# Spreading the last gate's adaLN rows over both MLP products, with their loads issued by GpSimd

## The chip, the core and the metric

The kernel runs on one core of a Trainium2 chip. Five engines of that core work side by side and meet only at semaphores: TensorE (PE; PEld is its weight load), VectorE (DVE), ScalarE (ACT), GpSimd (POOL) and SyncE (SP), which here only issues DMAs. Each runs its own list of instructions in a fixed order. The metric is the device time of one execution in microseconds (us). The times before are 1996.33, 1995.65 and 1997.18 us: a median of 1996.33.

## The reference, cut to what matters

One decoder layer on 512 tokens of width 2048, all in float32:

```python
mod = (c_act @ w_ada[l] + b_ada[l]).reshape(B, 6, D)
sh1, sc1, gt1, sh2, sc2, gt2 = [mod[:, j][:, None, :] for j in range(6)]
...
h = rmsnorm(x, g_norm_mlp[l]) * (1.0 + sc2) + sh2
hid = jnp.square(jax.nn.relu(jnp.einsum('bsd,df->bsf', h, w_mlp_in[l])))   # 2048 -> 8192
y = jnp.einsum('bsf,fd->bsd', hid, w_mlp_out[l])                           # 8192 -> 2048
x = x + gt2 * y
return rmsnorm(x, g_norm_final)
```

`gt2`, the last gate, is a product of the conditioning vector with 2048 columns of `w_ada`. Nothing needs it before the first finished columns of the second MLP product.

## The kernel before

**Arithmetic.** float32 products run as three matmuls each on a high and a low part (a*w = ah*wh + al*wh + ah*wl), so every weight tile is split first: ACT copies the high part, DVE subtracts it to get the low one (`low`, L122). Both MLP products use the Strassen-Winograd scheme: seven products instead of eight on half matrices. One **set** (one turn of the loop in `strassen`) loads one 512 KB weight tile `raw` (L1058, issued by SP), lets DVE form four sums of weights (L1060, L1067, L1068, tile `ts`), splits both (ACT L1066 and L1072; DVE L122, once 768 and once 1024 columns wide) and then runs 42 matmuls of 128x256 (L1102 to L1104) into seven PSUM banks.

**First product.** The hidden dimension is done in groups of 512 columns. Group 0 goes another way; groups 1 to 15 are 8 sets each. After a group, `combine` (one ACT copy, L1113, and seven DVE additions, L1114 to L1120) takes the seven banks apart; the next group needs those banks. There are eight. Squared-ReLU, splits and the sums for the second product follow in the background as `keep_parts` (L940, L948, L949: stores to DRAM issued by POOL) or, for the last two groups, `hold_parts` (kept in SBUF).

**Second product.** 13 parts of 8 to 16 sets (`parts`) walk over four blocks of output columns. A part that does not finish its block copies its seven banks out (L397 on ACT, L399 on DVE) and stores them as `prod` (L1300, POOL); a later part of the same block loads five of them back into tiles `n` (`load_pre`, L1239, POOL) and ACT puts them into the banks (L1090). The hidden activations come back from DRAM as pairs (`load_pair`, L1141 and L1144 on SP), split by ACT L1151 and DVE L122. The first three parts need no reload. The fourth part, 16 sets long, does the fourth block; the reload for the fifth part is asked for at its start.

**The last gate.** `ada_late` works through 64 **rows**: a row is a 128x512 tile of the transposed `w_ada` (256 KB), multiplied by the conditioning vector and summed by one DVE instruction (L1203). After every fourth row two tiny DVE instructions (L1208, L1209) finish 128 values of the gate. Three rows are loaded ahead (`LEAD`), into tiles `n`, of which there are five, in SP's queue. `ada_late` is a generator in the background lane `bg2`: each `tick()` (one per set) takes one off the lane's `wait`, and each row adds `pace[0]` to it, so the pace is in sets per row. `ensure(GT2)` runs what is left at once.

**Order.** The order on each engine comes from the tile framework's scheduler: it follows the program's order with priorities (`SETW` = 200 for the split of weights, `SETE` = 330 for `combine` and the copies out of the banks, rows at none) and its own estimate of when operands are there. DMAs under `keep_in_program_order` keep their order among themselves. The lines below show both functions and what calls them.

Of the kernel before, what the change touches and what calls it, by code (L numbers as in the profile page):

```python
# [16 lines left out]
P = 128  # L17
S = 512
D = 2048
NK = D // P  # L20
# [19 lines left out]
SH1, SC1, GT1, SH2, SC2, GT2 = range(6)  # L40
# [24 lines left out]
def hybrid_layer_kernel(  # L65
# [13 lines left out]
    nc = tc.nc  # L79
# [18 lines left out]
    def T(tag, dt=F32, cols=None):  # L98
        return new(next(split_tag) if tag == "w4" else tag, dt, cols)

    def new(tag, dt=F32, cols=None):
        count[0] += 1
        pool, bufs = (sp, BUFS[tag]) if tag in BUFS else pools[tag][:2]
        return pool.tile([P, cols or COLS[tag]], dt, tag=tag, name=f"{tag}_{count[0]}", bufs=bufs)

    def bank(tag):
        count[0] += 1
        return pp.tile([P, S], F32, tag=tag, name=f"ps_{tag}_{count[0]}", bufs=PBUFS[tag])
# [39 lines left out]
    def col(base, j):  # L148
        return vec[:, base + j : base + j + 1]
# [23 lines left out]
    for i in range(2):  # L173
        v = slice(i * S, (i + 1) * S)
        ps = bank("mm")
# [7 lines left out]
    def mod(m, j):  # L183
        return mods[:, m * NK + j : m * NK + j + 1]
# [80 lines left out]
    def blk(o):  # L265
        return slice(o * P, (o + 1) * P)


    class Lane:
# [8 lines left out]
        def next(self):  # L278
            if not self.queue:
                return False  # L280
            try:
                self.wait += next(self.queue[0]) or 0.0
            except StopIteration:
                self.queue.pop(0)
            return True
# [13 lines left out]
    bg, bgl, bg2 = Lane(), Lane(), Lane()  # L299

    def tick(dt=1.0):
        for lane in (bg, bgl, bg2):
            lane.run(dt)
# [137 lines left out]
    for o in range(8):  # L441
        t = T("a")
# [266 lines left out]
    pace = [3.2]  # L709

    def ensure(m):
        while m not in ready:
            assert bg2.next()
# [339 lines left out]
    def operands(src):  # L1053

        with tc.high_priority(offset=SETW):

            r = T("raw")
            nc.sync.dma_start(r.rearrange("p (c f) -> p c f", c=2), src)  # L1058
            t = T("ts")
            tt(  # L1060
                out=t[:, : 2 * HT].rearrange("p (a b) -> p a b", a=2),
                in0=r[:, HT : 3 * HT].rearrange("p (a b) -> p a b", a=2),
                in1=r[:, q_(0)].unsqueeze(1).broadcast_to([P, 2, HT]), op=ALU.add,
            )
            h, lo = T("w3", F32R), T("w3", F32R)
            act(h, r[:, HT:], AF.Copy)  # L1066
            tt(out=t[:, q_(2)], in0=t[:, q_(0)], in1=r[:, q_(2)], op=ALU.add)  # L1067
            tt(out=t[:, q_(3)], in0=t[:, q_(2)], in1=r[:, q_(3)], op=ALU.add)  # L1068
            low(lo, r[:, HT:], h)
            out = {n: (h[:, q_(i)], lo[:, q_(i)]) for i, n in enumerate(("11", "22", "21"))}  # L1070
            h, lo = T("w4", F32R), T("w4", F32R)
            act(h, t, AF.Copy)  # L1072
            low(lo, t, h)
            for i, n in enumerate(("t1", "t3", "t2", "t4")):
                out[n] = h[:, q_(i)], lo[:, q_(i)]
        return out
# [3 lines left out]

    loaded = [None]

    def strassen(src, acts, after=None, pre=None, before=None, js=range(8)):

        bs = [bank(next(turn)) for _ in PRODUCTS]
        if pre:
            n, ts = pre
            with tc.high_priority(offset=SETE):
                for b, t in zip(bs, ts):
                    act(b, t, AF.Copy)  # L1090
                for b, t in zip(bs[5:], load_pre(n, (5, 6), nc.scalar)):
                    act(b, t, AF.Copy)
        if before:
            loaded[0] = before()
        for j in js:
            w, a = operands(src(j)), acts(j)
            for b, (an, wn) in zip(bs, PRODUCTS):
                (ah, al), (wh, wl) = a[an], w[wn]
                for i in range(2):
                    out, st = b[:, q_(i)], j == js[0] and i == 0 and not pre  # L1100
                    kw = dict(skip_group_check=True)
                    mm(out, wh[:, blk(i)], ah, start=st, stop=False, **kw)  # L1102
                    mm(out, wh[:, blk(i)], al, start=False, stop=False, **kw)  # L1103
                    mm(out, wl[:, blk(i)], ah, start=False, stop=j == js[-1], **kw)  # L1104
            if after:
                after(j)
            tick()
        return bs
# [71 lines left out]
    at = itertools.count(-8)  # L1180

    def after_set():
        for f, p in todo.get(next(at), []):
            f(p)

    LEAD, row = 3, ["n"]

    def ada_late(m):

        def load(i):  # L1190
            t = T(row[0])
            tc.keep_in_program_order(nc.sync.dma_start(t, w_adaT[(m * NK + i // 4) * P : (m * NK + i // 4 + 1) * P, i % 4 * S : (i % 4 + 1) * S]))
            return t

        ts = [load(i) for i in range(LEAD)]
        for i in range(4 * NK):
            t, q = ts.pop(0), i % 4
            if i + LEAD < 4 * NK:
                ts.append(load(i + LEAD))
            yield pace[0]  # L1200
            if q == 0:
                ga = T("ga")
            stt(  # L1203
                out=t, in0=t, scalar=1.0, in1=cb[q // 2][:, q % 2 * S : (q % 2 + 1) * S], op0=ALU.mult, op1=ALU.mult,
                accum_out=ga[:, q : q + 1],
            )
            if q == 3:
                tt(out=ga[:, :2], in0=ga[:, :2], in1=ga[:, 2:4], op=ALU.add)  # L1208
                stt(  # L1209
                    out=mod(m, i // 4), in0=ga[:, 0:1], scalar=ga[:, 1:2], in1=col(C_BADA, m * NK + i // 4),  # L1210
                    op0=ALU.add, op1=ALU.add,
                )
        ready.add(m)

    pace[0] = 1.9
    w_pair = w_mlp_in.rearrange("(c k p) f -> k p c f", c=2, p=P)
    for g in range(1, NG):
        if g == 2:
# [2 lines left out]
        bs = strassen(lambda j: w_pair[j][:, :, g * 512 : (g + 1) * 512], acts_in, last, js=range(KP)[:: -1 if g == 1 else 1])  # L1221
# [5 lines left out]
        bg.add((keep_parts if g < NG - 2 else hold_parts)(g, *rs))  # L1227


    row[0] = "a"  # L1230
    prodD = [[dp.tile([P, S], F32, name=f"prod_{n}_{i}") for i in range(7)] for n in range(NO)]
    w_blocks = w_mlp_out.rearrange("(g c b p) d -> g b p c d", c=2, b=2, p=P)
    x2 = {}
# [2 lines left out]
    def load_pre(n, js, queue=nc.gpsimd):  # L1236
        ts = [T("n") for _ in js]
        for t, j in zip(ts, js):
            queue.dma_start(t, prodD[n][j])  # L1239
        return ts  # L1240
# [9 lines left out]
    nxt = None  # L1250
# [6 lines left out]
    for i, (n, ps) in enumerate(parts):  # L1257
        seen = {m for m, _ in parts[: i + 1]}
        left = [m for m, _ in parts[i + 1 :]]

        def before():
            if left and left[0] in seen:
                return left[0], load_pre(left[0], range(5))

        def after(p, n=n, early=(ps[4],) if n not in left and n < NO - 1 else ()):
            after_set()
            if p in early:
                load_x2(range(n * 4, n * 4 + 4), x1D)
            if i == len(parts) - 1 and p == ps[5]:
                load_x2(range(12, NK), x1D)  # L1270

        src = lambda q: w_blocks[ORDER[q] // 2][ORDER[q] % 2][:, :, n * 512 : (n + 1) * 512]
        bs = strassen(src, acts_out, after, nxt, before, ps)
        nxt = loaded[0]
        if n not in left:
            ensure(GT2)
            cs = [T("cb"), T("cb")]
            qs = [t[:, j * S : (j + 1) * S] for t in cs for j in range(2)]
            with tc.high_priority(offset=SETE):
                qs = combine(bs, *qs)  # L1280
            if n == NO - 1:
                for q, d in zip(qs, yD):
                    nc.gpsimd.dma_start(d, q)
                continue
            if acc2 is None:
                acc2 = T("a")
            with tc.high_priority(offset=SETW):
                for k, tok, q in quarters(n, *qs):
                    t = x2[k][:, tok]
                    stt(out=t, in0=q, scalar=mod(GT2, k), in1=t, op0=ALU.mult, op1=ALU.add)  # L1290
                for k, q in zip(range(n * 4, n * 4 + 4), qs):
                    add_square(acc2, x2[k], q, k == 0)
                    if n == 0:
                        nc.gpsimd.dma_start(x2D[k], x2[k])
        else:
            with tc.high_priority(offset=SETE):
                for j, b in enumerate(bs):
                    t = T("a")
                    copy(j + 1, t, b)
                    nc.gpsimd.dma_start(prodD[n][j], t)  # L1300
# [12 lines left out]
    for p in final:  # L1313
        t = T("a", F32R)
# [154 lines left out]
```

## Time and profile before

| | |
|---|---|
| median of three runs | 1996.33 us (1995.65 to 1997.18) |
| the profiled execution's own time | 1994.49 us |
| its span, first to last instruction | 1992.7 us |
| PE busy | 1941.9 us (97%) |
| DVE busy | 1760.6 us (88%) |
| ACT busy | 1074.6 us (54%) |
| POOL busy | 193.6 us (10%) |
| mean granted TensorE clock | 0.996 |
| moved by DMA | 443.51 MB, mean 223 GB/s |

The profile is one execution taken by the hardware profiler. "Busy" is a union of instruction times of one engine. In a window row, the number in brackets after an engine is its count of instructions in the window; a few matmul records can be missing. In a timeline row, the two first numbers are start and duration in us, and a bracket at the end tells how long the engine stood idle before it and what released it. The groups 1 to 15 of the first product run from about 760 to 1355 us, the second product from there to about 1960 us.

### The profile page before, as it was taken

The page shows a single profiled execution, that of the slowest core. Times are in us where ns is not written, and L with a number is a line of the kernel's source. Part 1 is how long each engine was busy: PE and PEld are TensorE (multiplying, and loading weights), DVE is VectorE, ACT ScalarE, POOL GpSimd, SP SyncE. Part 2 cuts the span into 40 slices and gives each one's busy share as a digit, 9 for nine tenths or more (in the row PEclk, how much of TensorE's full clock was granted, in tenths as well). Part 3 has the DMA queues.
Part 4 walks back from the last instruction along what each step waited for, and adds up shares of the span by engine and source line. Part 5 has one row for each costly group of instructions (what it writes and reads, how often), then busy time and mean ns, then how long its engine had stood idle before and what let it go on. Part 6 is the DMA issues. An engine that isn't in the chain of part 4 may idle for free. (4 is left out here: it accounts for less than half of the span.)

```text
span 1992.7 us, 37203 instructions
## 1 busy us (share of the span) xinstructions
PE 1941.9 (97%) x14148; PEld 1815.3 (91%) x14148; DVE 1760.6 (88%) x2979; ACT 1074.6 (54%) x1580; POOL 193.6 (10%) x307
## 2 busy tenths in 40 slices
PE   8999999999999998999999999999999999999997
PEld 6787887788888998999999999999999999999996
DVE  8998776988998599999999999999879779879996
ACT  5443564786433385555555555556445555556552
POOL 0000000000000000112111211200110210211100
PEclk9999999999999999999999999999999999999998
DMA  9896655556779544766666665755567668679653
GB/s 368 304 340 198 212 163 185 179 163 218 226 251 365 170 134 129 239 194 213 221 196 203 226 197 190 232 173 210 185 241 262 238 249 278 220 253 341 225 197 112
DMA packets 205238, 443.51 MB, mean 223 GB/s; under 512 B 20481, under 2 KB 42113, under 8 KB 205058
## 3 DMA queue, kind: packets, MB, share of 16 engines
q1 hardware_dynamic: 176338, 356.58, 54.2%
q0 software_dynamic: 23680, 77.61, 10.5%
q10 hardware_dynamic: 5040, 6.93, 1.0%
q8 instruction: 111, 1.82, 0.4%
q14 instruction: 69, 0.57, 0.1%
HBM read 376.30 MB, written 64.75 MB: 221 GB/s over the span
## 5 line engine op out<-in xcount | busy, mean ns | idle before, releaser
L1102 PE MATMUL ps_mm<-a,w 128*128 128x256 f32 x1696 | 469.1, 277 | 3.0 <-DVE a L1114 1.2
L1104 PE MATMUL ps_mm<-a,w 128*128 128x256 f32 x1696 | 469.2, 277 | 0.4 <-DVE w L122 0.3
L1103 PE MATMUL ps_mm<-a,w 128*128 128x256 f32 x1696 | 469.1, 277 | 0.4 <-DVE a L122 0.3
L1072 ACT ACTIVATE w<-ts 128x1024 fp32r<-128x1024 f32 x244 | 258.4, 1059 | 273.1 <-DVE ts L1068 241.5
L1104 PE MATMUL ps_z<-a,w 128*128 128x256 f32 x1304 | 362.0, 278 | 6.9 <-DVE w L122 6.8
L1102 PE MATMUL ps_z<-a,w 128*128 128x256 f32 x1304 | 362.2, 278 | 3.4 <-DVE a L1118 1.6
L1103 PE MATMUL ps_z<-a,w 128*128 128x256 f32 x1304 | 361.4, 277 | 0.1
L122 DVE TENSOR_TENSOR w<-ts,w 128x1024 fp32r<-128x1024 f32 x244 | 297.8, 1221 | 55.4 <-PE ps_mm L1103 20.4
L1102 PEld LDWEIGHTS ps_mm<-a,w 128*128 128x128 f32 x1696 | 318.4, 188 | 4.3 <-issue 2.5
L1104 PEld LDWEIGHTS ps_mm<-a,w 128*128 128x128 f32 x1696 | 318.7, 188 | 1.1 <-DVE w L122 1.0
L1103 PEld LDWEIGHTS ps_mm<-a,w 128*128 128x128 f32 x1696 | 318.7, 188 | 0.8 <-DVE a L122 0.8
L122 DVE TENSOR_TENSOR w<-raw,w 128x768 fp32r<-128x768 f32 (+1 forms) x296 | 267.5, 905 | 37.8 <-ACT w L244 24.0
L1066 ACT ACTIVATE w<-raw 128x768 fp32r<-128x768 f32 x244 | 204.5, 839 | 174.8 <-issue 80.5
L1104 PEld LDWEIGHTS ps_z<-a,w 128*128 128x128 f32 x1304 | 245.6, 189 | 8.2 <-DVE w L122 8.1
L1102 PEld LDWEIGHTS ps_z<-a,w 128*128 128x128 f32 x1304 | 245.8, 188 | 4.9 <-issue 2.1
L1103 PEld LDWEIGHTS ps_z<-a,w 128*128 128x128 f32 x1304 | 245.7, 188 | 0.6 <-DVE a L122 0.6
L244 ACT ACTIVATE wh<-wr 128x512 fp32r<-128x512 f32 (+1 forms) x184 | 113.2, 618 | 142.4 <-PE ps_mm L262 61.8
L1060 DVE TENSOR_TENSOR ts<-raw 128x512 f32<-128x512 f32 x244 | 166.8, 684 | 14.2 <-DMA raw<-in_w_mlp_out_dram 13.4
L259 PE MATMUL ps_mm<-a,wh 128*128 128x512 f32 x448 | 176.8, 395 | 2.6 <-DVE a L460 1.0
L263 PE MATMUL ps_mm<-a,wl 128*128 128x512 f32 x448 | 175.0, 391 | 1.5 <-DVE wl L122 1.3
L262 PE MATMUL ps_mm<-a,wh 128*128 128x512 f32 x448 | 174.9, 390 | 0.0
L211 DVE SCALAR_TENSOR_TENSOR x<-x,cb 128x1024 f32<-128x1024 f32 x108 | 131.2, 1218 | 23.4 <-DMA x<-in_w_adaT_dram 23.3
(336 smaller groups left out, 4007.7 us busy)
## 6 DMA issues: line engine op xcount, KB each, us to landing
raw<-in_w_mlp_out_dram SPq DMA_DIRECT2D x124, 512.0 KB, 4.6
raw<-in_w_mlp_in_dram SPq DMA_DIRECT2D x120, 512.0 KB, 3.8
x<-in_w_adaT_dram SPq DMA_DIRECT2D x108, 512.0 KB, 5.6
wr<-in_w_in_dram SPq DMA_DIRECT2D x160, 256.0 KB, 3.4
tt<-in_w_adaT_dram SPq DMA_DIRECT2D x52, 512.0 KB, 6.2
part<-a POOLq DMA_DIRECT2D x84, 256.0 KB, 3.9
a<-part SPq DMA_DIRECT2D x84, 256.0 KB, 6.3
prod<-a POOLq DMA_DIRECT2D x63, 256.0 KB, 5.8
```

What stands on the lines that cost most here:

```text
L122: tt(out=out, in0=full, in1=f32(high), op=ALU.subtract)
L211: ins = stt(out=t, in0=t, scalar=1.0, in1=cb[q_], op0=ALU.mult, op1=ALU.mult, accum_out=self.ga[:, q_ : q_ + 1],)
L244: act(h[:, :n], r[:, :n], AF.Copy)
L259: first = mm(out, wh, ah, start=start, stop=False, **kw)
L262: mm(out, wh, al, start=False, stop=False, **kw)
L263: mm(out, wl, ah, start=False, stop=stop, **kw)
L1060: tt(out=t[:, : 2 * HT].rearrange("p (a b) -> p a b", a=2), in0=r[:, HT : 3 * HT].rearrange("p (a b) -> p a b", a=2), in1=r[:, q_(0)].unsq ...
L1066: act(h, r[:, HT:], AF.Copy)
L1072: act(h, t, AF.Copy)
L1102: mm(out, wh[:, blk(i)], ah, start=st, stop=False, **kw)
L1103: mm(out, wh[:, blk(i)], al, start=False, stop=False, **kw)
L1104: mm(out, wl[:, blk(i)], ah, start=False, stop=j == js[-1], **kw)
```

## The change

Four things change, all around the 64 rows of the last gate:

- the pace in the first product is 2.7 sets per row instead of 1.9, and in the second product 1.3; at the start of the second product the lane waits 5 sets more;
- the row loads are issued by POOL instead of SP, always into tiles `n` (before, the last two went into tiles `a`);
- the reload for the fifth part is asked for at the 13th set of the fourth part instead of its first;
- `ensure(GT2)` moves from the first finished block to that reload.

```diff
-    def strassen(src, acts, after=None, pre=None, before=None, js=range(8)):
+    def strassen(src, acts, after=None, pre=None, before=None, js=range(8), at=0):
...
-        if before:
-            loaded[0] = before()
-        for j in js:
+        for n_, j in enumerate(js):
+            if before and n_ == at:
+                loaded[0] = before()
             w, a = operands(src(j)), acts(j)
...
-    LEAD, row = 3, ["n"]
+    LEAD, ROWS = 3, (2.7, 1.3)
...
-            t = T(row[0])
-            tc.keep_in_program_order(nc.sync.dma_start(t, w_adaT[...]))
+            t = T("n")
+            tc.keep_in_program_order(nc.gpsimd.dma_start(t, w_adaT[...]))
...
-    pace[0] = 1.9
+    pace[0] = ROWS[0]
...
-    row[0] = "a"
+    pace[0] = ROWS[1]
+    bg2.wait += 5.0
...
         def before():
             if left and left[0] in seen:
+                ensure(GT2)
                 return left[0], load_pre(left[0], range(5))
...
-        bs = strassen(src, acts_out, after, nxt, before, ps)
+        bs = strassen(src, acts_out, after, nxt, before, ps, 12 if i == 3 else 0)
         nxt = loaded[0]
         if n not in left:
-            ensure(GT2)
```

Because a scheduler sets the order, the diff does not tell where instructions end up. Three places show it. The first is DVE at the end of group 10 of the first product, up to the first addition of `combine` (L1114). `n_...` with L1203 is a row, `w_...` a split of weights. Before:

```order
L122 TENSOR_TENSOR w_2326_12785<-raw_12780,w_2325_12784 128x768
L1060 TENSOR_TENSOR ts_12857<-raw_12855 128x512
L1203 SCALAR_TENSOR_TENSOR n_12978,ga_13161<-n_12978,cb_82 128x512
L1067 TENSOR_TENSOR ts_12857<-ts_12857,raw_12855 128x256
L1068 TENSOR_TENSOR ts_12857<-ts_12857,raw_12855 128x256
L122 TENSOR_TENSOR w_2328_12791<-ts_12782,w_2327_12790 128x1024
L122 TENSOR_TENSOR w_2337_12860<-raw_12855,w_2336_12859 128x768
L1114 TENSOR_TENSOR a_12763<-ps_z_12256,a_12761 128x512
```

and now:

```order
L122 TENSOR_TENSOR w_2312_12743<-raw_12738,w_2311_12742 128x768
L1060 TENSOR_TENSOR ts_12815<-raw_12813 128x512
L1067 TENSOR_TENSOR ts_12815<-ts_12815,raw_12813 128x256
L1068 TENSOR_TENSOR ts_12815<-ts_12815,raw_12813 128x256
L122 TENSOR_TENSOR w_2314_12749<-ts_12740,w_2313_12748 128x1024
L122 TENSOR_TENSOR w_2323_12818<-raw_12813,w_2322_12817 128x768
L1114 TENSOR_TENSOR a_12721<-ps_z_12217,a_12719 128x512
```

The row that stood five instructions ahead of the combine is gone from this stretch. Between the combines of groups 1 to 15 DVE's list had 3, 8, 7, 4, 4, 4, 5, 4, 4, 4, 4, 5, 4 and 2 rows (the first number is what stands ahead of group 2's combine); now it has 3, 6, 3, 3, 3, 3, 3, 3, 3, 3, 3, 3, 7 and 1. Of the rows that are left, 17 come in the second product, in bunches.

The second place is POOL's queue at the end of the third part of the second product, from the last store of that part's banks on. Before:

```order
L1300 DMA prod_6_15434<-a_16962 128x512
L1239 DMA n_16972<-prod_0_15428 128x512
L1239 DMA n_16973<-prod_1_15429 128x512
L1239 DMA n_16974<-prod_2_15430 128x512
L1239 DMA n_16975<-prod_3_15431 128x512
L1239 DMA n_16976<-prod_4_15432 128x512
L1300 DMA prod_0_15435<-a_18006 128x512
```

and now:

```order
L1301 DMA prod_6_15371<-a_16935 128x512
L1192 DMA n_17004<-in_w_adaT_dram 128x512
L1192 DMA n_17074<-in_w_adaT_dram 128x512
L1192 DMA n_17199<-in_w_adaT_dram 128x512
L1192 DMA n_17268<-in_w_adaT_dram 128x512
L1192 DMA n_17339<-in_w_adaT_dram 128x512
L1240 DMA n_17760<-prod_0_15365 128x512
L1240 DMA n_17761<-prod_1_15366 128x512
L1240 DMA n_17762<-prod_2_15367 128x512
```

The last five rows' loads stand between the stores and the reload. All five tiles `n` are in use by them, so the first reload (`n_17760`) takes the tile of the row `n_17004` and waits until DVE has worked on it.

The third place is ACT at the same time, around the first L1090, which reads that reload. Before:

```order
L1066 ACTIVATE w_2964_17174<-raw_17170 128x768
L1072 ACTIVATE w_2966_17180<-ts_17172 128x1024
L1090 ACTIVATE ps_mm_18027<-n_16972 128x512
L1239 DMA n_18039<-prod_5_15433 128x512
L1066 ACTIVATE w_2970_17230<-raw_17226 128x768
L1072 ACTIVATE w_2972_17236<-ts_17228 128x1024
```

and now:

```order
L1072 ACTIVATE w_2957_17152<-ts_17144 128x1024
L1066 ACTIVATE w_2962_17205<-raw_17201 128x768
L1072 ACTIVATE w_2964_17211<-ts_17203 128x1024
L1090 ACTIVATE ps_mm_18027<-n_17760 128x512
L1066 ACTIVATE w_2974_17274<-raw_17270 128x768
L1240 DMA n_18039<-prod_5_15370 128x512
L1072 ACTIVATE w_2976_17280<-ts_17272 128x1024
```

The L1090 stands one set later in ACT's list than before (after the splits of the 30th set instead of the 29th), ahead of the next set's split of weights.

More of the change, by code (lines that the diff above doesn't have):

```diff
@@ L1184, in after_set @@
             f(p)
-    LEAD, row = 3, ["n"]
+    LEAD, ROWS = 3, (2.7, 1.3)
     def ada_late(m):
         def load(i):
-            t = T(row[0])
-            tc.keep_in_program_order(nc.sync.dma_start(t, w_adaT[(m * NK + i // 4) * P : (m * NK + i // 4 + 1) * P, i % 4 * S : (i % 4 + 1) * S]))
+            t = T("n")
+            tc.keep_in_program_order(nc.gpsimd.dma_start(t, w_adaT[(m * NK + i // 4) * P : (m * NK + i // 4 + 1) * P, i % 4 * S : (i % 4 + 1) * S]))
             return t
```

## The prediction

> **What bounds the kernel now.** I read the page's first part, then windows by stage, then waits and timelines at the places where PE stands still.
>
> ```profile
> PE 1941.9 (97%) x14148; PEld 1815.3 (91%) x14148; DVE 1760.6 (88%) x2979; ACT 1074.6 (54%) x1580; POOL 193.6 (10%) x307
> ...
> 822.00:1345.00 523.00, 518.13 (x4534) 515.40 (x4533) 514.82 (x885) 286.66 (x380) 90.72 (x133) 1.00 0.64 207
> 1345.00:1395.00 50.00, 47.35 (x399) 46.02 (x398) 48.50 (x79) 31.26 (x46) 0.56 (x1) 1.00 0.60 210
> 1395.00:1475.00 80.00, 80.00 (x708) 80.00 (x707) 67.09 (x103) 36.48 (x46) 11.24 (x21) 1.00 0.51 172
> 1475.00:1500.00 25.00, 25.00 (x223) 25.00 (x222) 18.55 (x27) 13.57 (x18) 2.18 (x4) 1.00 1.04 384
> 1500.00:1530.00 30.00, 30.00 (x268) 30.00 (x267) 29.69 (x47) 16.75 (x24) 0.00 (x0) 1.00 0.85 303
> ...
> 1395.00:1825.00 430.00, 430.00 (x3797) 1.00 0.71 249
> ```
>
> The columns are window, length, busy time (count) of PE, PEld, DVE, ACT and POOL, granted clock, DMA share, GB/s (the last row: PE alone). PE bounds the kernel, so only its gaps can be won. From 1395 to 1825 us it has none: 3797 matmuls in 430 us, 0.1133 us each. At that rate 822 to 1345 us (groups 2 to 14 with the rows) would hold 4618 matmuls; it holds 4534, so 84 x 0.1133 = **9.5 us** are lost there, and by the same count **4.8 us** in the passage to the second product (1345 to 1395). In both DVE is 97 to 98% busy; in the second product it has room (67 of 80 us), but not at 1500 to 1530.
>
> Fifteen-us windows around the ends of groups (PE alone) show where the 9.5 us lie:
>
> ```profile
> 882.00:897.00 15.00, 13.73 (x116) 1.00 0.44 135
> 922.00:937.00 15.00, 13.92 (x113) 1.00 0.36 112
> 998.00:1013.00 15.00, 15.00 (x135) 1.00 0.42 123
> 1036.00:1051.00 15.00, 14.88 (x132) 1.00 0.40 124
> 1153.00:1168.00 15.00, 14.44 (x126) 1.00 0.39 117
> 1191.00:1206.00 15.00, 15.00 (x135) 1.00 0.41 119
> 1229.00:1244.00 15.00, 14.75 (x129) 1.00 0.38 109
> 1307.00:1322.00 15.00, 14.51 (x128) 1.00 0.40 118
> ```
>
> These are 8 of 13, the ends of groups 2 to 14; the others, from 842, 960, 1075, 1114 and 1269 on, hold 130, 134, 129, 134 and 127. Full is about 134.5. In all 82 matmuls are missing (9.3 us), so the loss is at the ends of groups and nowhere else. DVE's list tells the ends apart: where a row stands within the seven instructions ahead of the combine (9 ends; of the rows shown 882, 922, 1153 and 1307) 73.5 are missing, 8.2 each or 0.93 us; where none does (998, 1036, 1191, 1229) 0, 2.5, 0 and 5.5, or **0.23 us** each. One of the bad ends on DVE and on PE:
>
> ```profile
> 884.26 0.68 DVE L1203 SCALAR_TENSOR_TENSOR n<-n,cb 128x512 f32<-128x512 f32 x1
> 884.87 0.08 DVE L1203 DVE_READ_ACCUMULATOR n<-n,cb 128x1 f32 x1
> 886.88 0.68 DVE L1114 TENSOR_TENSOR a<-ps_o,a 128x512 f32<-128x512 f32 x1
> ...
> 887.62 0.38 PE L1102 MATMUL ps_o<-a,w 128*128 128x256 f32 x1 [0.49 <-DVE a L1114]
> 891.04 0.36 PE L1102 MATMUL ps_z<-a,w 128*128 128x256 f32 x1 [0.54 <-DVE a L1118]
> ```
>
> DVE reaches the combine without a pause, so it comes late, and PE waits for its banks (L1114, L1118).
>
> **The change part by part.**
>
> *Rows moved out of the first product.* A row holds DVE for 0.61 us (from 884.26 to 884.87); L1208 and L1209 add about 0.2 us per four rows, so 0.66 us. By the lists, groups 3 to 13 have 36 rows instead of 53: 17 x 0.66 = 11 us less for DVE, 1 us per group, in a stage where it has 1.6%. Seven of these eleven ends had a row close ahead of the combine and now none has. They miss 62.5 matmuls, 7.1 us; at 0.23 us each they would lose 1.6. **Gain 5.5 us.** The least: PE's idle time alone at these seven (15.00 less 13.73, 13.92, 14.44 and so on) is 3.7 us, of which 3.1 go (the four ends without a row keep 0.09 each); the most is 7.1 plus the 0.9 of the four others, 8.0. I take 5.5, and 0.4 for those four, since the rows are thinner there too.
>
> *Group 14 gets more.* Seven rows instead of four stand ahead of its combine, three of them among the last nine instructions. It is like groups 3 and 4, which had 8 and 7 and lost 18.5 and 21.5 matmuls, 2.1 and 2.4 us; group 14 lost 6.5 (0.7 us). **Loss 1.2 us**, between 0 and 1.7.
>
> *The passage.* Two row loads leave SP's queue and a time of full DMA; POOL's loads for the rows nearby are issued earlier, when the tiles come free.
>
> ```profile
> 1340.63 0.42 SPq L1192 DMA_DIRECT2D n<-in_w_adaT_dram  x1
> 1345.36 0.42 SPq L1058 DMA_DIRECT2D raw<-in_w_mlp_out_dram  x1
> 1346.48 0.33 SPq L1192 DMA_DIRECT2D n<-in_w_adaT_dram  x1
> ...
> 1338.00:1352.00 14.00, 14.00 (x126) 14.00 (x125) 12.86 (x22) 5.94 (x8) 0.00 (x0) 1.00 0.94 326
> ...
> 1351.87 0.69 DVE L1060 TENSOR_TENSOR ts<-raw 128x512 f32<-128x512 f32 x1 [1.11 <-DMA raw<-in_w_mlp_out_dram]
> 1352.48 0.69 DVE L1203 SCALAR_TENSOR_TENSOR n<-n,cb 128x512 f32<-128x512 f32 x1
> 1353.89 1.22 DVE L122 TENSOR_TENSOR w<-ts,w 128x1024 fp32r<-128x1024 f32 x1
> ...
> 1353.26 0.39 PE L1102 MATMUL ps_z<-a,w 128*128 128x256 f32 x1 [1.00 <-ACT a L1113]
> 1355.85 0.36 PE L1102 MATMUL ps_mm<-a,w 128*128 128x256 f32 x1 [1.16 <-DVE a L1114]
> ```
>
> 256 KB at 326 GB/s is 0.8 us, so `raw` lands 0.8 us or, with SP's 0.42, up to 1.2 us sooner than 1351.87. Right ahead of L1114 stood that wait, the row and the 1024-wide split (1.22 us); the row goes, and in the new list the split comes after L1116. PE's two waits (2.2 us of the 4.8) shrink; what is late next is that split. **Gain 2.2 us**; from 0, if the split then stops PE as long, to 3.5.
>
> *Rows in the second product.* 17 rows, 11 us of DVE, in bunches behind the first three parts. At 1395 to 1475 us DVE is idle 13 us and POOL's list loads these rows well ahead: nothing. What covers it is weights split ahead; without that a bunch of six costs 4 us. The last five rows meet the reload:
>
> ```profile
> 1473.10 0.55 POOL L1239 DMA_DIRECT2D n<-prod  x1
> 1475.44 0.55 POOL L1239 DMA_DIRECT2D n<-prod  x1 [1.79 <-DMA prod<-a]
> ...
> n<-prod POOLq DMA_DIRECT2D x45, 256.0 KB, 6.9
> n<-in_w_adaT_dram SPq DMA_DIRECT2D x62, 256.0 KB, 4.2
> ...
> 1480.28 0.60 ACT L1090 ACTIVATE ps_mm<-n 128x512 f32<-128x512 f32 x1 [3.55 <-DMA n<-prod]
> 1484.40 0.85 ACT L1066 ACTIVATE w<-raw 128x768 fp32r<-128x768 f32 x1 [1.26 <-PE ps_mm L1103]
> ...
> 1502.71 1.22 DVE L122 TENSOR_TENSOR w<-ts,w 128x1024 fp32r<-128x1024 f32 x1
> ...
> 1504.94 0.28 PE L1104 MATMUL ps_o<-a,w 128*128 128x256 f32 x1
> ```
>
> Before, the reload was issued at 1473.10 and ACT stood 3.55 us for it, until 1480.28, at no cost to PE. Now the row's load takes that slot (SP's lands in 4.2 us at the median, POOL's reload in 6.9: 1477.9 to 1480.6 with 0.55 to issue), DVE works 0.6 us, and the reload needs 0.55 + 6.9: 1486 to 1488.7. Behind the waiting L1090 on ACT stands the split that began at 1484.40: it comes 2.2 to 4.9 us late, DVE's low part and the next load of `raw` behind it. The cover is thin: matched by order, the split that DVE finishes at 1503.93 is read by PE at 1504.94, and DVE, full from 1500 to 1530, can't catch up. So PE stands 1.2 to 3.9 us, less what DVE's 6.4 idle us at 1475 to 1500 take. **Loss 1.6 us**, from 0 to 4.
>
> *Issue by POOL.* 64 issues of 0.55 us (what `n<-prod` takes) on an engine that is 10% busy: nothing. They queue behind stores, but three rows ahead at 2.7 sets of 42 x 0.1133 us is 38 us. SP loses 62 issues it had time for.
>
> The Trainium skill (page "SBUF — State Buffer", section "Who interferes with whom") has a rule that speaks against this: a DVE instruction with two SBUF inputs contends with a GpSimd instruction that reads SBUF, and whichever is second blocks, though it infers that writing descriptors needs the other interface; its section "SBUF: two separate sides" advises the hardware queues for that. I weigh it as a rival below.
>
> Sum: 5.5 + 0.4 - 1.2 + 2.2 - 1.6 = 5.3 us. The profiled execution took 1994.49 us (span 1992.7), so 1989.2 for it; the median of the runs is 1.84 us above it, so 1996.33 - 5.3 = **1991.0 us**.
>
> **The rivals.** *The ends of groups don't care for rows.* The loss could lie in the combine itself, eight steps through one spare bank, and 1229 lost 5.5 matmuls without a row. Against: 998 and 1191. Then 5.9 shrinks to about 1 and the sum is 1 - 0 + 1.5 - 1.6: **1995.4 us**.
>
> *Everything is won.* All ends but group 14's fall to nothing (9.3 - 0.7 - 1.2), the passage gives 2.2 and the reload costs nothing: 9.6 us, **1986.7 us**. For it: two ends without a row lose 0 today. Against: two loads, one behind the other, in a time of full DMA.
>
> *The reload stops PE, and the kernel is slower.* In a time of 384 GB/s both loads may take the longest that a tile `n` took, 9.3 us:
>
> ```profile
> DMA to landing us min/median/max: 3.1/5.1/9.3
> ```
>
> 1473.65 + 9.3 + 0.6 + 0.55 + 9.3 = 1493.4; the split is 9.6 us late instead of 4.9, PE stands 8.6 us. With the least gain at the ends (3.1 - 1.2) and none in the passage that is 6.7 us more: **2003.0 us**. It decides from a first L1090 at about 1492 on, where the 1.0 us of cover and the other parts' gain of 6.9 are used up.
>
> *DVE and POOL block each other.* If each issue held DVE for 0.55 us, 47 rows in the first product, where DVE has no room, would cost 26 us less the 5.3: **2017 us**. But POOL issued 84 stores of `part` there, and they landed as fast as SP's loads of one size, beside DVE instructions that never stretched:
>
> ```profile
> part<-a POOLq DMA_DIRECT2D x84, 256.0 KB, 3.9
> ...
> L1060 DVE TENSOR_TENSOR ts<-raw x244: 675/684/696, 754.4 to 1935.5; 128x512 f32<-128x512 f32 x122
> ```
>
> The rule of the page, as it may be read for descriptors, is this rival; the trace bears out its inference.
>
> **How the numbers follow.** 0.2% is 4 us, about what a measurement of this kernel can tell from no change: faster is below 1992.3. Forecast 0.5, and within it (1988 to 1994.5) about 0.7 below the line; ends that don't care 0.25 (one in ten below); all won 0.15; reload 0.08; blocking 0.02. Faster: 0.35 + 0.03 + 0.15 = 0.53. Slower: 0.10. Same: 0.37. The range leaves out the two dear rivals and reaches to the other two: 1986.5 to 1997.5.
>
> **What would show it.** Right: 822 to 1345 us holds some 45 matmuls more, the ends of groups 3 to 13 about 134, the end of group 14 fewer than 128; DVE is near 96% there; the passage lacks about 20 matmuls instead of 42; the first L1090 starts at 1486 to 1489 on today's clock of the stage and PE has a gap of 1 to 4 us in the 20 us behind it. Wrong: ends of groups that lack as many as now with DVE idle before L1114 (the combine itself), a gap of over 5 us in the fourth part (the reload), or L1060 above 0.7 us (blocking).

## The result, and the profile after

The changed kernel takes **2012.60 us** (median of 6 runs, 2006.79 to 2015.79), the kernel before 1996.76 us beside it (6 runs). The ratio is **1.0075, with a 95% interval from 1.0063 to 1.0087**: slower by about 15 us, where the prediction had 1991.0 us and gave "slower" one chance in ten. The profiled execution took 2012.64 us, its span is 2010.8 us.

The first part of the page and the stages of the changed kernel, with the prediction's windows (window, length, busy time and count of PE, PEld, DVE, ACT and POOL, granted clock, DMA share, GB/s):

```profile
PE 1946.4 (97%) x14148; PEld 1818.3 (90%) x14148; DVE 1762.0 (88%) x2979; ACT 1076.0 (54%) x1580; POOL 229.2 (11%) x371
...
822.00:1345.00 523.00, 508.50 (x4419) 504.53 (x4418) 496.12 (x831) 282.25 (x373) 117.10 (x180) 1.00 0.62 198
...
1500.00:1530.00 30.00, 27.24 (x234) 26.70 (x234) 25.87 (x45) 15.69 (x23) 1.09 (x2) 1.00 1.01 375
1530.00:1825.00 295.00, 295.00 (x2605) 295.00 (x2605) 244.27 (x355) 163.19 (x219) 38.95 (x72) 1.00 0.70 250
```

The work is the same; PE does it in 18 us more. Between 822 and 1345 us it starts 4419 matmuls, 115 fewer than before: at 0.1133 us each, 13.0 us. The prediction wanted some 45 more there. And DVE is *less* busy, 496.12 us of 523 instead of 514.82, more than the thinner rows explain. An engine that was full now stands still, so the next view is what it waits for. DVE's waits between 822 and 1345 us of the changed kernel (what waited, what released it: us in total, times, longest):

```profile
DVE n L1203 <- DMA n<-in_w_adaT_dram: 20.1, 12, 3.2
DVE w L122 <- ACT w L1072: 2.4, 12, 0.2
```

and the same of the kernel before:

```profile
DVE w L122 <- ACT w L1072: 2.6, 13, 0.2
DVE n L1203 <- DMA n<-in_w_adaT_dram: 2.5, 6, 0.8
```

The rows (L1203) wait for their loads 20.1 us instead of 2.5. What POOL, which now issues these loads, waits for between 800 and 1345 us:

```profile
POOL part L940 <- ACT a L126: 268.0, 25, 25.7
POOL sum L949 <- DVE a L948: 58.2, 40, 8.3
```

POOL stands most of the stage at the next store in its list, up to 25.7 us at a time, and whatever is queued behind that store stands with it. One group on POOL, on DVE and on PE shows the rest:

```profile
945.55 0.58 POOL L1192 DMA_DIRECT2D n<-in_w_adaT_dram  x1 [1.45 <-issue]
946.11 0.71 POOL L940 DMA_DIRECT2D part<-a  x1
946.69 0.70 POOL L1192 DMA_DIRECT2D n<-in_w_adaT_dram  x1
...
950.01 0.68 POOL L1192 DMA_DIRECT2D n<-in_w_adaT_dram  x1
950.57 0.83 POOL L949 DMA_DIRECT2D sum<-a  x1
977.07 0.68 POOL L940 DMA_DIRECT2D part<-a  x1 [25.67 <-ACT a L126]
```

```profile
952.62 0.68 DVE L1203 SCALAR_TENSOR_TENSOR n<-n,cb 128x512 f32<-128x512 f32 x1
...
953.56 0.68 DVE L1203 SCALAR_TENSOR_TENSOR n<-n,cb 128x512 f32<-128x512 f32 x1
...
957.53 0.69 DVE L1203 SCALAR_TENSOR_TENSOR n<-n,cb 128x512 f32<-128x512 f32 x1 [2.94 <-DMA n<-in_w_adaT_dram]
...
958.15 1.22 DVE L122 TENSOR_TENSOR w<-ts,w 128x1024 fp32r<-128x1024 f32 x1
...
959.43 0.39 PE L1104 MATMUL ps_mm<-a,w 128*128 128x256 f32 x1 [1.60 <-DVE w L122]
```

The three loads of a group leave within 4.5 us, when the stores around them come free. Their rows stand in DVE's list right behind, 7.1, 6.9 and 7.5 us after the issue. The third has not landed: DVE stands 2.94 us, the weight split (L122) queued behind it is late, and PE waits 1.60 us. DVE's wait for the third row comes back in every group from 4 to 14, 0.3 to 3.2 us long. The Trainium skill (page "DMA: Bandwidth & Descriptors", section "Anatomy of one DMA — SWDGE (gpsimd) path") states that a DMA's wait for a semaphore is made by the issuing sequencer ahead of the dispatch; the 25.67 us agree.

In the fourth part of the second product the last five rows do something like it. There DVE stands 3.7 us for three of them and ACT 3.27 us for the reload (L1090, first at 1501.02 us), and PE loses 3.9 us between 1499 and 1523 us by the gaps between its matmuls. The longest is this one; just ahead of it DVE stood 3.14 us for a `raw`, until 1512.91 us:

```profile
1517.27 0.39 PE L1104 MATMUL ps_o<-a,w 128*128 128x256 f32 x1 [2.45 <-DVE w L122]
```

### The profile page after: what moved, and what is told of

Read it like the earlier page. It is cut to its first block, busy times and chain, and to the rows that moved or that the text cites. A ratio compares the mean times of both kernels' runs of the same rounds, so it can differ in the third digit from the quotient of the medians.

```text
span 2010.8 us, 37187 instructions
## 1 busy us (share of the span) xinstructions
PE 1946.4 (97%) x14148; PEld 1818.3 (90%) x14148; DVE 1762.0 (88%) x2979; ACT 1076.0 (54%) x1580; POOL 229.2 (11%) x371
## 5 line engine op out<-in xcount | busy, mean ns | idle before, releaser
L122 DVE TENSOR_TENSOR w<-ts,w 128x1024 fp32r<-128x1024 f32 x244 | 297.9, 1221 | 41.5 <-PE ps_mm L1104 15.6
L122 DVE TENSOR_TENSOR w<-raw,w 128x768 fp32r<-128x768 f32 (+1 forms) x296 | 267.5, 905 | 43.0 <-ACT w L244 25.4
L1060 DVE TENSOR_TENSOR ts<-raw 128x512 f32<-128x512 f32 x244 | 167.0, 685 | 11.9 <-DMA raw<-in_w_mlp_out_dram 11.4
```

What stands on the lines that cost most here:

```text
L122: tt(out=out, in0=full, in1=f32(high), op=ALU.subtract)
L1060: tt(out=t[:, : 2 * HT].rearrange("p (a b) -> p a b", a=2), in0=r[:, HT : 3 * HT].rearrange("p (a b) -> p a b", a=2), in1=r[:, q_(0)].unsq ...
```

## The experiments

Three accounts stood at the start. **A**: POOL's queue makes the loads late, and rows are placed right behind them. **B**: the paces themselves (rows in threes, the later reload) cost the time, whoever issues. **C**: an issue by POOL holds DVE up, the prediction's rival of 2017 us. The times of before differ a little from one set of runs to the next; each ratio is against its own.

### The changed kernel, loads by SP again

```diff
-            tc.keep_in_program_order(nc.gpsimd.dma_start(t, w_adaT[...]))
+            tc.keep_in_program_order(nc.sync.dma_start(t, w_adaT[...]))
```

> The changed kernel with one word put back: the row loads are issued by SP again. Theory A (POOL's queue): in the changed kernel a row load stands behind stores of part and sum that wait up to 25.7 us for ACT, three loads go out together, and DVE, whose list has the rows 3 to 7 us behind them, stands 20.1 us for them in the first product. With SP that wait falls to 4 us or less, 822 to 1345 us holds at least as many matmuls as before the change (4534), and the time is 1988 to 1997 us. Theory B (the paces and places): rows in threes and the later reload cost the time whoever issues the loads: DVE still waits over 10 us or the ends of groups lose more, and the time stays within 4 us of 2012. Theory C (an issue by POOL holds DVE): the time falls as in A, but by the number of issues (64 of 0.55 us or more), not by the waits of L1203.

Measured: 1992.08 us, ratio 0.9982 (0.9973 to 0.9991). The one word is worth 19 to 21 us (by the ratios and by the medians), and the rest of the change is a gain. DVE's list of waits in the first product no longer has the rows among its six longest. That stage and three of the ends of its groups (PE alone in the last three rows):

```profile
822.00:1345.00 523.00, 521.57 (x4595) 520.84 (x4594) 512.85 (x857) 292.64 (x385) 90.72 (x133) 1.00 0.62 204
...
996.00:1011.00 15.00, 15.00 (x135) 1.00 0.39 122
1148.00:1163.00 15.00, 15.00 (x135) 1.00 0.36 119
1300.00:1315.00 15.00, 15.00 (x135) 1.00 0.38 120
```

4595 matmuls are 61 more than before, or 6.9 us; the ends are full, group 14's (1300) too. B is out for the first product. A and C both fit. But the fourth part now loses 5.5 us by PE's gaps between 1479 and 1502 us (with a granted clock of 0.57 from 1498 to 1502), and DVE's waits from 1395 to 1530 us point at the rows:

```profile
DVE n L1203 <- DMA n<-in_w_adaT_dram: 13.4, 6, 6.0
```

### The kernel before, loads by POOL

```diff
-            tc.keep_in_program_order(nc.sync.dma_start(t, w_adaT[...]))
+            tc.keep_in_program_order(nc.gpsimd.dma_start(t, w_adaT[...]))
```

> The kernel before with one word changed: its row loads are issued by POOL; the paces stay at 1.9 and the reload stays where it was. Theory A: DVE waits for rows 15 us or more between 822 and 1345 us (2.5 before), and the time is 2004 to 2015 us. Theory B: the paces are what costs, so it stays within 4 us of the kernel before. The difference from the changed kernel is then what the paces and the place of the reload are worth behind POOL's queue.

Measured: 2008.52 us, ratio 1.0065 (1.0048 to 1.0082). The issuer alone makes the old kernel slower by 13 us. The size of the wait was expected higher:

```profile
DVE n L1203 <- DMA n<-in_w_adaT_dram: 11.6, 10, 2.5
```

### The changed kernel, six rows ahead

```diff
-    LEAD, ROWS = 3, (2.7, 1.3)
+    LEAD, ROWS = 6, (2.7, 1.3)
...
-            t = T("n")
+            t = T("a")
```

> The changed kernel with six rows loaded ahead instead of three, into tiles a (there are only five tiles n); POOL still issues. Rival to theory A's details: three rows ahead are simply too few, and twice as many carry the rows over POOL's standstill: DVE's wait for rows falls under 4 us and the time to 1988 to 1997 us. Theory A as it reads in the trace: the scheduler pulls a row forward to where its own estimate has the load landed, however many are ahead, so the row follows its load by 3 to 8 us all the same: DVE waits 10 us or more, and the time stays at 2003 us or above.

Measured: 2027.24 us, ratio 1.0167 (1.0149 to 1.0185). More depth does not help: DVE still waits 23.1 us for rows. It makes things worse in a way that none of the accounts had, because rows in tiles `a` push into the tiles that wait for their own stores:

```profile
DVE a L1203 <- DMA a<-in_w_adaT_dram: 23.1, 16, 3.5
DVE a L948 <- DMA part<-a: 11.9, 9, 5.9
```

So its time says nothing on A alone; its 23.1 us do say that loading twice as many rows ahead does not bring them in time: a row still starts 5.7 us behind its load at the median of the stage (loads and rows paired in order).

### Loads by SP, the reload early

```diff
 (from the kernel with SP's loads)
-    LEAD, ROWS = 3, (2.7, 1.3)
+    LEAD, ROWS, row = 3, (2.7, 1.3), ["n"]
...
-            t = T("n")
+            t = T(row[0])
...
+    row[0] = "a"          # row tiles of the second product
...
-                ensure(GT2)
...
-        bs = strassen(src, acts_out, after, nxt, before, ps, 12 if i == 3 else 0)
+        bs = strassen(src, acts_out, after, nxt, before, ps, 0)
         nxt = loaded[0]
         if n not in left:
+            ensure(GT2)
```

> The changed kernel with loads by SP, and the reload for the fifth part asked for at the first set of the fourth part as before the change; the rows of the second product go into tiles a so that the two don't share tiles. Against the run with SP alone it tells what the place of the reload is worth. If the reload behind the last five rows costs PE the 3.9 us that the trace of the changed kernel shows at 1499 to 1522 us, this one is 2 to 4 us faster than the run with SP alone and has no gap over 1 us in the fourth part. If that loss was POOL's queue too, both are within 1 us of each other.

Measured: 1997.92 us, ratio 1.0011 (0.9998 to 1.0023): 5.8 us *slower* than the run above, where it was to be 2 to 4 us faster. All waits between 1475 and 1500 us:

```profile
ACT w L1072 <- DVE ts L1068: 11.8, 3, 8.3
DVE a L1203 <- DMA a<-in_w_adaT_dram: 11.2, 2, 9.7
...
PE ps_o L1104 <- DVE w L122: 5.1, 1, 5.1
...
ACT ps_mm L1090 <- DMA n<-prod: 2.4, 1, 2.4
```

ACT's wait for the reload is 2.4 us; what stops PE for 5.1 us is a row that DVE waits 9.7 us for, with a split of weights behind it. So an early reload does not cure this stage while rows stand in it. (The tiles changed with it, and the reload's loads now run at the same time as the rows', so the price of the reload alone was not isolated.)

### Loads by SP, rows end early

```diff
 (from the kernel with SP's loads)
-    LEAD, ROWS = 3, (2.7, 1.3)
+    LEAD, ROWS = 3, (2.7, 0.9)
```

> The run with SP's loads, with one number changed: 0.9 sets per row in the second product instead of 1.3, so that the last row comes at its 19th set by DVE's list and not at its 32nd. With SP's loads PE lost 5.5 us from 1479 to 1502 us, where DVE stood 6.0, 1.0 and 4.1 us for rows whose loads share the DMA with the pair loads that start at 1462 us. If those four late rows are the cause, the fourth part loses under 1.5 us and the time is 1986 to 1990 us (1992.1 before). If it is the reload or the pair loads themselves, or if the rows cost as much in the third part, it stays within 1.5 us of 1992.1.

Measured: 1987.11 us, ratio 0.9954 (0.9942 to 0.9967). With the last row ahead of the fourth part, 1395 to 1530 us holds 1188 matmuls; with 1.3 sets it held 1143, here in this order:

```profile
1395.00:1530.00 135.00, 134.57 (x1188) 1.00 0.73 256
```

```profile
1395.00:1530.00 135.00, 131.91 (x1143) 0.99 0.74 258
```

45 matmuls are 5.1 us, which is the difference of the two times. So it was the rows in the fourth part. What ended early with them is also their hold on the tiles `n` that the reload needs: the first L1090 starts at 1473.30 us instead of 1499.59, and the two are not parted.

### The changed kernel, rows kept in order

```diff
-            stt(
+            later(stt(
                 out=t, in0=t, scalar=1.0, in1=cb[...], op0=ALU.mult, op1=ALU.mult,
                 accum_out=ga[:, q : q + 1],
-            )
+            ))
```

`later` keeps an instruction in the program's order on its engine. POOL issues, in the same order as in the changed kernel but for one load, which stands behind seven stores of `prod` instead of ahead of them.

> The changed kernel, POOL still issues all 64 row loads in the same places of its queue, but the rows themselves are kept in the program's order on DVE, so that the scheduler can't pull a row up to right behind its load: by DVE's list each row now stands three rows behind its load. If the loss is rows that stand 3 to 8 us behind loads that POOL issues late (theory A as the first four runs left it), DVE's wait for rows in the first product falls from 20.1 to under 4 us, 822 to 1345 us holds over 4570 matmuls as with SP (4595), and the time is 1988 to 1998 us although POOL issues; 23 rows instead of 17 then come in the second product, and if POOL's stores of prod hold their loads there, that is where up to 5 us stay. If an issue by POOL as such slows DVE or PE (theory C), it stays above 2004 us.

Measured: 1987.91 us, ratio 0.9958 (0.9944 to 0.9972). This is the run that settles it. The load that POOL issued at 945.55 us above goes out at 945.68 here, but its row starts at 985.80, 40 us later instead of 7.1. DVE's wait for rows and the stage:

```profile
DVE n L1203 <- DMA n<-in_w_adaT_dram: 2.5, 1, 2.5
```

```profile
822.00:1345.00 523.00, 522.16 (x4595) 521.21 (x4595) 511.89 (x849) 291.79 (x384) 116.07 (x179) 1.00 0.65 206
```

POOL still stands at its stores (219.1 us for ACT's splits of `part`, 268.0 in the changed kernel), and it costs almost nothing, since no row of this stage but the first follows its load closely. That first one, 6.5 us behind its load, is the 2.5 us, and the end of its group (2) loses 1.8 us. Against the changed kernel this is 23 to 25 us (by the ratios and by the medians). Six rows more have left for the second product, but by the prediction's 0.66 us a row that is only 4 us of DVE. C has little left to explain. In the fourth part PE still loses 3.8 us. Up to 5 were allowed for there, but by late loads, and DVE waits for no row: seven rows stand in it from 1481 to 1515 us, where it is full (28.70 of 30 us from 1500 on), and ACT waits 3.4 us for the reload.

### Rows kept in order, SP or POOL, 2.7 or 2.3 sets

The edits above combined: rows kept, 0.9 sets in the second product, loads by SP.

> As the run that ends early, with the rows kept in the program's order on DVE. Tells what the scheduler's pulling forward is worth where the queue is not the trouble: the eight rows ahead of the third group's combine become three (that end lost 2.06 us), so the first product gains up to 2 us; 23 rows come in the second product, the last at its 26th set, 2 sets into the fourth part. Expected 1985 to 1990 us; if rows in the fourth part cost whatever their place, 1989 to 1993.

Measured: **1983.16 us, ratio 0.9936 (0.9924 to 0.9948), the lowest of all**, under the range expected and faster than both kernels. 4609 of the 4618 matmuls that fit start between 822 and 1345 us. Then with 2.3 sets per row in the first product:

> As the one before, with 2.3 sets per row in the first product: 3 or 4 rows per group instead of 3, and 16 in the second product, the last at its 19th set. If three rows per group are what lets the ends of groups go unhurt (no group of four), the first product loses 2 to 5 us against the run with 2.7; if rows are free as long as none stands right ahead of a combine, it loses under 1 us and this is the fastest of the four, 1984 to 1989 us.

Measured: 1986.27 us, ratio 0.9946 (0.9934 to 0.9958). The groups with four rows are not hurt (PE is busy 513.00 of the 513 us from 822 to 1335); what is left of a difference lies in the passage, where PE loses 3.9 us between 1340 and 1347 us: a gap of 2.05 us, and then a granted clock of 0.57 from 1343 to 1347. It is not the fastest, but the two intervals overlap. And with POOL as the issuer again, 2.7 and 0.9 sets:

> The fastest kernel so far (SP, rows kept in order, 2.7 and 0.9) with the loads issued by POOL again: the issuer alone, where nothing is placed right behind its load. Theory A: the issuer by itself costs nothing, so the time is within 0.15% (3 us) of 1983.2, with DVE's wait for rows under 4 us in the first product. Theory C, in what is left of it: 64 issues cost DVE or PE something small but real, and the time is 1987 us or more.

Measured: 1985.09 us, ratio 0.9953 (0.994 to 0.9967): 1.9 us above SP's by the medians and 3.4 by the ratios, each against its own kernel before, with overlapping intervals. So 64 issues by POOL cost nothing that these runs can tell from zero. What the trace has of a price is again the first row: DVE waits 1.6 us for it and the end of group 2 loses 1.4 us, where with SP it loses nothing. And DVE's sums of weights (L1060) are no longer than in any other run:

```profile
L1060 DVE TENSOR_TENSOR ts<-raw x244: 679/685/695, 753.3 to 1923.7; 128x512 f32<-128x512 f32 x122
```

### The kernel before, rows kept in order

The same `later(stt(...))` in the kernel before: 1.9 sets, loads by SP.

> The kernel before with the rows kept in the program's order on DVE and nothing else changed: 1.9 sets per row, loads by SP, 4 or 5 rows in every group, 6 rows left for the second product. It parts the gain of the fastest kernel into keeping the order and thinning the rows. If the ends of groups lose because there are too many rows in a stage where DVE has 1.6% of room (the prediction's account), this one stays within 4 us of the kernel before. If they lose because the scheduler drops rows right ahead of the combine, the ends of groups 3 to 14 lose under 3 us in all (7.4 before) and the time falls to 1988 to 1992 us.

Measured: 1993.66 us, ratio 0.9998 (0.9987 to 1.0009). Neither branch holds as a whole. The ends of groups do heal without a single row less: from the combine of group 1 to that of group 14 it takes 500.6 us instead of 507.4, 6.8 us won. Ends with a row 3.4 to 3.6 us ahead of the combine lose 0 to 0.8 us; at those from 1029 and 1067 us it stands four instructions ahead and no matmul is missing:

```profile
1029.00:1044.00 15.00, 15.00 (x135) 1.00 0.41 123
1067.00:1082.00 15.00, 15.00 (x135) 1.00 0.42 121
```

The passage gives 4.4 us of it back: group 15 takes 47.0 us instead of 42.5. There `raw`, issued at 1341.38 us, is ready at 1348.11, and PE stands twice:

```profile
1346.33 0.39 PE L1104 MATMUL ps_z<-a,w 128*128 128x256 f32 x1 [2.91 <-DVE w L122]
1350.47 0.55 PE L1102 MATMUL ps_mm<-a,w 128*128 128x256 f32 x1 [2.56 <-DVE a L1114]
```

Behind them the granted clock is 0.54 from 1350 to 1355 us. (The trace is of an execution of 1990.90 us; its span is 3.5 us shorter than that of the kernel before, a gain that the median does not show.) So the order won the ends of groups. In the passage the fastest kernel takes 42.5 us for group 15 and the one with 2.3 sets 44.3; that thinner rows are what helps there fits, but the lane's wait of five sets and the later reload differ too. Why `raw` is late there (the rows' and pairs' loads ahead of it in SP's queue, DMA at 400 GB/s) was not tried apart.

## Why the prediction was wrong, by its own steps

**The step that failed: *Issue by POOL*, put at "nothing".** Its 0.55 us per issue was nearly right (0.68 in the trace) and beside the point. Its cover, "three rows ahead at 2.7 sets of 42 x 0.1133 us is 38 us", was read from `LEAD` in the code. `LEAD` says how many loads may be out; it does not say when a row runs. The scheduler, which leaves rows without a priority, had moved the rows up to just behind their loads (to where it held them for landed, as we read it; that it moved them is what keeping their order showed). The lists of the two engines showed it: the loads of `n_10241`, `n_10427` and `n_10546` are POOL's last of a group, and their rows stand within seven instructions of each other on DVE, next to the sums whose stores surround those loads. The true distance, with loads and rows paired in order, is 7.7 us at the median of the stage and 4.4 to 7.5 us for the rows that DVE stood for, with 5.8 us to land at the median. With SP's loads the rows are moved up too, but less: 13.1 us behind their loads in the kernel before and 15.6 in the changed one. Between 1395 and 1475 us, where DVE has room, it waits 3.5 us for three rows too, and no gap of PE follows: *Rows in the second product* held there. Measured, *Issue by POOL* is a loss of 19 to 21 us (the changed kernel against the one with SP) or 13 us (the kernel before).

**Rows moved out of the first product** (5.5 + 0.4 us, group 14 -1.2, together 4.7). With SP's loads the stage holds 61 matmuls more, 6.9 us: right in sign and near in size. Group 14 was too dear: with SP's loads three rows stand ahead of its combine and its end is full; the seven came with POOL's order, and there PE's gaps from 1318 to 1331 us cost 4.6 us. The *reason* was only half right. That an end with a row within seven instructions of the combine loses 0.93 us falls with the kernel before with rows kept: most ends with a row about four instructions ahead lose under 0.2 us. The ends that lost most before, 887 and 927 us, have five and six rows in the last 14 us, and so has the one end that the run with SP's loads still lost (888 us, six rows, 2.06 us); where rows are spread, three to five in a group cost nothing at most ends and 0.8 us at the worst. That is a reading, not shown: ends of the kernel before with two to four rows in that stretch lost 0 to 0.9 us, and nothing here varied the bunching alone.

**The passage** (2.2 us): 405 matmuls in the 50 us from 1356.4 us on, which is the same place 11.4 us later, so 36 are missing instead of 42: 0.7 us.

**The reload** (-1.6 us, 0 to 4). The first L1090 was to start at 1486 to 1489 us; it starts at 1501.02, 1489.6 when the 11.4 us are taken off, and PE loses 3.9 us: within its range. Its chain (the reload, ACT's split, DVE's low part, the next `raw`) was only part of it, for DVE stands 3.7 us for rows first. The two were not parted in one run, but either is seen without the other: with SP's loads ACT does not wait for the reload, DVE waits 11.1 us for rows between 1475 and 1505 us and PE loses 5.5 us; with POOL and rows kept DVE waits for no row (it is full), ACT waits 3.4 us for the reload and PE loses 3.8 us. With the rows ended early it costs nothing.

**The rivals.** "DVE and POOL block each other" came nearest in time (2017 us) and is not what happened: L1060 keeps its 684 ns in the changed kernel, and 64 issues by POOL cost nothing that can be told from zero once rows are spread. No rival had a row that waits for its load in the first product.

## What to carry to other kernels

A DMA that is to come early needs a queue with nothing in it that waits: behind stores that wait for another engine's result, a load goes out when they do (here a store stood for up to 25.7 us), whatever the engine's busy share says (11% here). How far a load runs ahead of its use is read from the two engines' lists side by side, not from the depth in the source, because a scheduler may pull the use up to the load. A consumer that shares an in-order engine with the critical work can be pinned late instead: kept in program order, the same loads from the same queue went from 15 us lost to 8 or 9 us won here.

## What the runs showed of the hardware that was not expected

A stall of PE can be paid twice. After the wait of 2.52 us at 1156.01 us in the changed kernel the granted clock falls to half for about 3 us:

```profile
1153.00:1156.00 3.00, 0.49 (x5) 1.00 0.09 36
1156.00:1157.00 1.00, 0.99 (x8) 1.00 0.08 16
1157.00:1158.00 1.00, 1.00 (x8) 0.64 0.17 25
1158.00:1159.00 1.00, 1.00 (x7) 0.50 0.65 139
1159.00:1160.00 1.00, 1.00 (x6) 0.50 0.86 332
1160.00:1161.00 1.00, 1.00 (x8) 0.65 0.08 29
1161.00:1162.00 1.00, 1.00 (x11) 1.00 0.65 90
```

The gap itself is 2.69 us, the whole cluster costs 4.39. With SP's loads a gap of 1.98 us at 1495.5 us was followed by 0.58 over 3 us, and in the run with 2.3 sets one of 2.05 us at 1341 us by 0.57 over 4 us; in the changed kernel one of 2.61 us at 1514.5 us was followed by 1.00, and so was one of 3.84 us at 962.5 us in the run with six rows ahead. So length alone does not decide it here. The Trainium skill (page "TensorE: Matmul & The Clock Gate", section "What's actually happening") has half clock after an idle window of about 3.4 us that runs freely. The half, and its 3 us, agree with this trace; that gaps of 2.0 to 2.7 us were enough in these three runs does not agree with a whole idle window.
